# Grouping heads by bank in a causal attention step: four heads for the first 128 tokens, two for the next, one for the rest

## Chip, cores and metric

The kernel runs on one core of one Trainium2 chip. The metric is the device time of one execution in microseconds (us). Before the change it is 1768.77 us, the median of 3 runs (1768.34 to 1769.28).

## The reference

Two layers of a decoder trunk work on one sequence of 512 tokens with 1024 channels, all in float32. Each layer is a SwiGLU block, a token mixer and a second SwiGLU block. The mixer runs a causal convolution over half of its channels and a differential attention with four heads over the other half. Differential attention forms two softmax maps per head and subtracts the second, scaled, from the first:

```python
def diff_attention(q, k, v, rel_bias, lam, lam_init, subln_g):
    # q, k: (B, H, 2, S, d); v: (B, H, S, 2d); H = 4, S = 512, d = 64; 128-query blocks
    ...
        s = jnp.einsum("bhmqd,bhmkd->bhmqk", qi, k).astype(jnp.float32) * scale
        s = s + bias[None, :, None]
        s = jnp.where((dist >= 0)[None, None, None], s, -1e30)
        p = jax.nn.softmax(s, axis=-1)
        a = p[:, :, 0] - lam * p[:, :, 1]
        return jnp.einsum("bhqk,bhkd->bhqd", a.astype(v.dtype), v)
    ...
    o = rms_norm(o, subln_g) * (1.0 - lam_init)

def reference(...):
    for l in range(DEPTH):                      # 2
        x = x + 0.5 * swiglu(rms_norm(x, ffn1_norm[l]), ...)
        a, g, q, k, v = jnp.split(rms_norm(x, mix_norm[l]) @ w_in[l], splits, axis=-1)
        conv_out = conv_module(a, g, conv_w[l], conv_b[l], conv_norm[l])
        ...
        diff_out = diff_attention(q, k, v, rel_bias, lam, lam_init, subln_norm[l])
        x = x + jnp.concatenate([conv_out, diff_out], axis=-1) @ w_out[l]
        x = x + 0.5 * swiglu(rms_norm(x, ffn2_norm[l]), ...)
    return x
```

## The kernel before

The activations stay on the chip. Weights are streamed from memory and split into two parts each, so that large products run as several passes on the tensor engine (PE). Nearly all of the time goes to the SwiGLU blocks. The change touches the function `mixer` alone, which runs once per layer.

In `mixer`, queries, keys and values are projected, normalised and turned into `qz`, `kt` and `vv`. The 512 tokens are four blocks of 128 queries, numbered `i` = 0 to 3. Block `i` looks only at the first `W = (i + 1) * 128` keys, so a score product for one head and one of its two maps is 128 x W: 512 columns for the last block, 384, 256, and 128 for the first.

The attention is a pipeline of steps. Before, a step is one block and one head, 16 steps in all, with the last block first (`steps`). The function `attend(n)` issues the score and softmax work of step n (`softmaxes`), the transposes of step n - 2 (`keys_first`), the value products of step n - 3 (`values`), and the output of a block five steps behind its last head (`block_out`).

- `softmaxes` (L949): two score products, one for each map (L958), into two banks of PSUM, the tensor engine's output memory. A bank holds 512 float32 values per partition. For each map, VectorE (DVE) adds the bias and finds a running minimum (L962), and ScalarE (ACT) takes the exponential and its sum (L966). The first map goes to the tile `e0`, the second stays in its bank. A reciprocal (L969) and a small product (L971) form the factor, and L972 adds the scaled second map to the first.
- `keys_first` (L975): i + 1 transposes of 128 x 128 on PE into one bank (L979), and one ACT copy of all of them to `at` (L981).
- `values` (L984): i + 1 products for the head (L988) into its quarter of a bank that all four heads share. After the last head come the norm of the block (L995 to L1003) on ACT, DVE and GpSimd (POOL).
- `block_out` (L1011): four transposes (L1015), an ACT copy (L1017) and a DVE operation (L1018) that write the block's part of the output projection's input.

The banks come from tags, with a number of buffers each. The score banks have the tags `sc` and `po`, two buffers each; the block outputs have `mm`, two; the transposes `tp`, one; the convolution and the row sums `y`, one:

```python
    BANKS = {"mm": 2, "sc": 2, "po": 2, "tp": 1, "y": 1}

    def bank(tag, name):
        return psum.tile([P, 512], F32, tag=tag, name=name, bufs=BANKS[tag])
```

The pipeline stands between the value projection and the output projection (`ps_out`, L200 to L204 and L1065), which uses the banks `sc` and `po` too. The projection works first on the attention half for the later 256 tokens, then on the convolution half for all tokens, then on the attention half for the first 256. The convolution's taps (L902 to L931) and its norm (L933 to L943) run on DVE, ACT and POOL during the attention.

Each engine runs its instructions in a fixed order. A planner makes that order when the program is built: it walks the program with estimated durations and gives a free engine the ready instruction that stands earliest in program order, except where an order is pinned. It also places the semaphores between engines.

Of the kernel before, what the change touches and what calls it, by code (L numbers as in the profile page):

```python
# [23 lines left out]
NT = SEQ // P  # L24
# [7 lines left out]
HEADS = 4  # L32
HD = 64
VD = 2 * HD
# [36 lines left out]
def trunk(ctx: ExitStack, tc: tile.TileContext, xt, par, lamv, relb, onehot,  # L71
          gu1, dn1, wag, wqkv, wout, gu2, dn2, out):
    nc = tc.nc
    V, S, G, T = nc.vector, nc.scalar, nc.gpsimd, nc.tensor

    const = ctx.enter_context(tc.tile_pool(name="const", bufs=1))
    small = ctx.enter_context(tc.tile_pool(name="small", bufs=2))
# [11 lines left out]
    def bank(tag, name):  # L89
        return psum.tile([P, 512], F32, tag=tag, name=name, bufs=BANKS[tag])  # L90
# [121 lines left out]
    for l in range(DEPTH):  # L212
        pt = const.tile([P, NPAR], F32, tag=f"par{l}", name=f"par{l}")
# [572 lines left out]
    def mixer(l, pr, after, begun):  # L786
        with tc.tile_pool(name="mix", bufs=1) as mp, tc.tile_pool(name="mt", bufs=2) as mt:
# [155 lines left out]
                    V.scalar_tensor_tensor(cl[:, c, :], z, hg, f32(ch[:, c, :]), op0=ALU.mult, op1=ALU.subtract)  # L943


            steps = [(i, h) for i in reversed(range(NT)) for h in range(HEADS)]
            sums, pos, maps, ats = {}, {}, {}, {}

            def softmaxes(i, h):  # L949
                W = (i + 1) * P  # L950
                tq = slice(i * P, W)
                if h == 0:
                    sums[i] = small.tile([P, 2, HEADS], F32, tag="sums", name="sums")
                scs = [bank(tag, "ps_sc")[:, :W] for tag in ("sc", "po")]
                e0 = mt.tile([P, SEQ], F32, tag="e0", name="e", bufs=4)[:, :W]
                sm = sums[i]
                for m in range(2):
                    T.matmul(scs[m], qz[:, m, h, tq], kt[:, h, :W], start=True, stop=True)  # L958

                for m, (sc, e) in enumerate(zip(scs, (e0, scs[1]))):  # L960
                    mn = small.tile([P, 1], F32, tag=f"mn{m}", name="mn")
                    V.tensor_tensor_reduce(  # L962
                        out=e, in0=sc, in1=bias[:, h, SEQ - W :], scale=1.0, scalar=3e38,
                        op0=ALU.add, op1=ALU.min, accum_out=mn,
                    )
                    S.activation(e, e, AF.Exp, bias=mn, scale=-1.0, accum_out=sm[:, m, h : h + 1])  # L966

                r2 = small.tile([P, 1], F32, tag="r2", name="r2")
                V.reciprocal(r2, sm[:, 1, h : h + 1])  # L969
                c2 = small.tile([P, 1], F32, tag="c2", name="c2")  # L970
                V.tensor_scalar(c2, r2, nlam[l], sm[:, 0, h : h + 1], op0=ALU.mult, op1=ALU.mult)  # L971
                V.scalar_tensor_tensor(e0, scs[1], c2, e0, op0=ALU.mult, op1=ALU.add)  # L972
                maps[i, h] = e0

            def keys_first(i, h):  # L975
                pt = bank("tp", "ps_at")
                for j in range(i + 1):
                    t = slice(j * P, (j + 1) * P)
                    T.transpose(pt[:, t], maps[i, h][:, t], ident)  # L979
                at = mt.tile([P, SEQ], F32, tag="at", name="at")  # L980
                S.activation(at[:, : (i + 1) * P], pt[:, : (i + 1) * P], AF.Copy)  # L981
                ats[i, h] = at

            def values(i, h):  # L984
                if h == 0:
                    pos[i] = bank("mm", "ps_o")
                for j in range(i + 1):
                    T.matmul(pos[i][:, h * VD : (h + 1) * VD], ats[i, h][:, j * P : (j + 1) * P], vv[:, j, h, :],  # L988
                             start=j == 0, stop=j == i)
                if h < HEADS - 1:  # L990
# [31 lines left out]
            def attend(n):  # L1022
                if n < len(steps):
                    softmaxes(*steps[n])
                if 2 <= n < len(steps) + 2:
                    keys_first(*steps[n - 2])
                if 3 <= n < len(steps) + 3:
                    values(*steps[n - 3])
                if n >= 5 and steps[n - 5][1] == HEADS - 1:
                    block_out(steps[n - 5][0])  # L1030

            for c in range(CT - 1):
# [157 lines left out]
```

## Time and profile before

| | |
|---|---|
| median of 3 runs | 1768.77 us (1768.34 to 1769.28) |
| the profiled execution | 1769.0 us, its span 1767.2 us |
| granted PE clock | 1.00 |
| PE busy | 1758.8 us, 11852 matmul rows |
| DVE busy | 1472.1 us, 2646 instructions |
| ACT busy | 1037.1 us, 1955 instructions |
| POOL busy | 515.7 us, 497 instructions |
| first score product of the attention, layer 1 and 2 | 452.0 us, 1329.5 us after the start |

A row of the profile names the line of the kernel, the engine, the operation, the tiles written and read, the shape, and how often it came. Times are from one profiled execution. A float32 score product appears as two PE rows. Rows of PE overlap, since a product starts while the one before it is draining, so distances between starts say more of PE's speed than durations. "Idle before" names the time for which an engine had nothing running ahead of an instruction, and what ended it.

### The profile page before, as it was taken

The numbers are of one execution on the slowest core, as the hardware profiler recorded it, in microseconds if no ns is written. First come the engines' busy times: TensorE is split into PE (matmuls) and PEld (weight loads), VectorE is DVE, ScalarE is ACT, GpSimd is POOL, SyncE is SP. The second block draws the span as 40 slices with busy tenths as digits, with TensorE's granted clock in tenths as the row PEclk, the third lists the DMA queues.
The fourth block names the chain that finished last, engine by engine and source line by source line (L and its number), as shares of the span: only waits on it lengthen the run. The fifth ranks groups of instructions, "written<-read, shape, count | busy, mean of one in ns | idle before, by whom it ended". The sixth has DMA issues, their size and how long they took to land.

```text
span 1767.2 us, 32964 instructions
## 1 busy us (share of the span) xinstructions
PE 1758.8 (100%) x11852; PEld 1621.2 (92%) x11852; DVE 1472.1 (83%) x2646; ACT 1037.1 (59%) x1955; POOL 515.7 (29%) x497
## 2 busy tenths in 40 slices
PE   9999999999999999999999999999999999999998
PEld 7799999988788899999988999999887888999998
DVE  7969888969877969989987798999698678698887
ACT  6546566755865436566644565666559554465664
POOL 1011112169970011212200121121798600112122
PEclk9999999999999999999999999999999999999999
DMA  7457777533223457677544576776231234576774
GB/s 229 129 138 185 172 188 190 138 120 100 68 78 114 126 129 178 171 198 179 141 143 111 147 177 172 198 166 166 91 114 49 96 102 139 134 183 163 201 183 127
DMA packets 166613, 257.78 MB, mean 146 GB/s; under 512 B 19271, under 2 KB 63318, under 8 KB 166448
## 3 DMA queue, kind: packets, MB, share of 16 engines
q1 hardware_dynamic: 129600, 201.25, 35.5%
q0 software_dynamic: 36416, 54.12, 18.7%
q8 instruction: 93, 1.52, 0.4%
q14 instruction: 72, 0.59, 0.1%
q10 hardware_dynamic: 432, 0.29, 0.1%
HBM read 253.48 MB, written 3.42 MB: 145 GB/s over the span
## 4 chain that ended last, share of the span: by engine, by line
PE 97%; DVE 1%; POOL 1%; ACT 1%; issue 0%; DVEq 0%; POOLq 0%
PE ps_pair L434 37%; PE ps_pair L523 18%; PE ps_pair L200 9%; PE ps_pair L203 9%; PE ps_pair L204 9%; PE ps_out L200 2%; PE ps_out L203 2%; PE ps_out L204 2%; PE ps_pair L842 2%; PE ps_pair L843 2%; PE ps_pair L841 2%; PE ps_sc L958 1%; PE ps_v L872 1%; PE ps_v L873 1%; PE ps_v L871 1%; POOL wlo L102 0%
## 5 line engine op out<-in xcount | busy, mean ns | idle before, releaser
L101 ACT ACTIVATE whi<-wraw 128x512 fp32r<-128x512 f32 x744 | 452.9, 627 | 397.4 <-PE ps_pair L203 166.3
L102 DVE TENSOR_TENSOR wlo<-wraw,whi 128x512 fp32r<-128x512 f32 x640 | 426.2, 685 | 111.5 <-ACT whi L101 104.2
L160 POOL DMA_DIRECT2D wsum<-in_gu x128 | 112.0, 904 | 700.4 <-DMA wsum<-in_gu 270.7
L434 PE MATMUL ps_pair<-acth,wlo 128*128 128x256 f32 x1024 | 289.8, 283 | 0.0
L434 PE MATMUL ps_pair<-actl,whi 128*128 128x256 f32 x1024 | 289.8, 283 | 0.0
L434 PE MATMUL ps_pair<-acth,whi 128*128 128x256 f32 x1024 | 289.8, 283 | 0.0
L434 PE MATMUL ps_pair<-th,whi 128*128 128x256 f32 x768 | 217.3, 283 | 0.0
L434 PE MATMUL ps_pair<-tl,whi 128*128 128x256 f32 x768 | 217.3, 283 | 0.0
L434 PE MATMUL ps_pair<-th,wlo 128*128 128x256 f32 x768 | 217.3, 283 | 0.0
L200 PE MATMUL ps_pair<-acth,whi 128*128 128x512 f32 x512 | 200.7, 394 | 0.3 <-DVE gs L653 0.3
L203 PE MATMUL ps_pair<-actl,whi 128*128 128x512 f32 x512 | 199.7, 390 | 0.0
L204 PE MATMUL ps_pair<-acth,wlo 128*128 128x512 f32 x512 | 199.3, 390 | 0.0
L434 PEld LDWEIGHTS ps_pair<-actl,whi 128*128 128x128 f32 x1024 | 196.6, 192 | 0.2
L434 PEld LDWEIGHTS ps_pair<-acth,whi 128*128 128x128 f32 x1024 | 196.6, 192 | 0.2
L434 PEld LDWEIGHTS ps_pair<-acth,wlo 128*128 128x128 f32 x1024 | 196.6, 192 | 0.0
L160 POOL DMA_DIRECT2D wsum<-in_dn x112 | 98.9, 1112 | 269.4 <-DMA wsum<-in_dn 55.7
L434 PEld LDWEIGHTS ps_pair<-th,whi 128*128 128x128 f32 x768 | 147.5, 192 | 0.0
L434 PEld LDWEIGHTS ps_pair<-tl,whi 128*128 128x128 f32 x768 | 147.5, 192 | 0.0
L434 PEld LDWEIGHTS ps_pair<-th,wlo 128*128 128x128 f32 x768 | 147.5, 192 | 0.0
L102 POOL TENSOR_TENSOR wlo<-wraw,whi 128x512 fp32r<-128x512 f32 x104 | 137.4, 1345 | 30.4 <-ACT whi L101 19.4
L523 PE MATMUL ps_pair<-hh,whi 128*128 128x256 f32 x512 | 144.9, 283 | 0.0
L523 PE MATMUL ps_pair<-hl,whi 128*128 128x256 f32 x512 | 144.9, 283 | 0.0
(209 smaller groups left out, 4446.5 us busy)
## 6 DMA issues: line engine op xcount, KB each, us to landing
wraw<-in_gu SPq DMA_DIRECT2D x280, 256.0 KB, 3.4
wsum<-in_gu SPq DMA_DIRECT2D x128, 256.0 KB, 3.7
wsum<-in_gu POOLq DMA_DIRECT2D x128, 256.0 KB, 4.7
wraw<-in_dn SPq DMA_DIRECT2D x68, 256.0 KB, 3.4
wraw<-in_wqkv SPq DMA_DIRECT2D x48, 256.0 KB, 2.7
wraw<-in_wout SPq DMA_DIRECT2D x48, 256.0 KB, 2.7
wraw<-in_dn SPq DMA_DIRECT2D x64, 128.0 KB, 4.0
wraw<-in_wag SPq DMA_DIRECT2D x32, 256.0 KB, 3.0
```

Of the source, the lines that this page charges most:

```text
L101: S.activation(hi, raw, AF.Copy)
L102: (eng or V).tensor_tensor(out=lo, in0=raw, in1=f32(hi), op=ALU.subtract)
L160: nc.gpsimd.dma_start(dst[:, to], src, accum_op=ALU.add)
L200: first = T.matmul(ps, wh, xh, start=start, stop=False)
L203: T.matmul(ps, wh, xl, start=False, stop=False)
L204: T.matmul(ps, wl, xh, start=False, stop=stop)
L434: mm = T.matmul(ps, l, r, start=first and i == j == 0, stop=False, skip_group_check=True)
L523: mm = T.matmul(ps, s[:, f], r, start=side not in self.begun, stop=False, skip_group_check=True)
L841: T.matmul(ps[n], xh[:, t], wh, start=k == 0, stop=False)
L842: T.matmul(ps[n], xh[:, t], wl, start=False, stop=False)
L843: T.matmul(ps[n], xl[:, t], wh, start=False, stop=k == KT - 1)
L871: T.matmul(ps, xh[:, t], wh, start=k == 0, stop=False)
```

## The change

A step becomes one block and a range of heads: one head for the blocks of 512 and 384 keys, two heads for the block of 256, four for the block of 128. There are 11 steps per layer instead of 16. All heads of a step share the two score banks, one tile `e0`, one bank of transposes, one copy and one pair of reciprocal and product. Bias, exponential and combination are still issued once for each head and map. The small product is now a scalar-tensor-tensor operation on as many columns as there are heads, and the minima have four buffers per map instead of two. The distances in `attend` are the same in steps.

```diff
-            steps = [(i, h) for i in reversed(range(NT)) for h in range(HEADS)]
+            steps = []
+            for i in reversed(range(NT)):
+                g = (4, 2, 1, 1)[i]
+                steps += [(i, range(h, h + g)) for h in range(0, HEADS, g)]
...
-            def softmaxes(i, h):
-                W = (i + 1) * P
+            def softmaxes(i, hs):
+                W, g = (i + 1) * P, len(hs)
...
-                scs = [bank(tag, "ps_sc")[:, :W] for tag in ("sc", "po")]
-                e0 = mt.tile([P, SEQ], F32, tag="e0", name="e", bufs=4)[:, :W]
+                scs = [
+                    bank(tag, "ps_sc")[:, : g * W].rearrange("p (n w) -> p n w", n=g) for tag in ("sc", "po")
+                ]
+                e0 = mt.tile([P, SEQ], F32, tag="e0", name="e", bufs=4)[:, : g * W]
+                e0 = e0.rearrange("p (n w) -> p n w", n=g)
                 sm = sums[i]
                 for m in range(2):
-                    T.matmul(scs[m], qz[:, m, h, tq], kt[:, h, :W], start=True, stop=True)
+                    for n, h in enumerate(hs):
+                        T.matmul(scs[m][:, n], qz[:, m, h, tq], kt[:, h, :W], start=True, stop=True)
 
                 for m, (sc, e) in enumerate(zip(scs, (e0, scs[1]))):
-                    mn = small.tile([P, 1], F32, tag=f"mn{m}", name="mn")
-                    V.tensor_tensor_reduce(
-                        out=e, in0=sc, in1=bias[:, h, SEQ - W :], scale=1.0, scalar=3e38,
-                        op0=ALU.add, op1=ALU.min, accum_out=mn,
+                    for n, h in enumerate(hs):
+                        mn = small.tile([P, 1], F32, tag=f"mn{m}", name="mn", bufs=4)
+                        V.tensor_tensor_reduce(
+                            out=e[:, n], in0=sc[:, n], in1=bias[:, h, SEQ - W :], scale=1.0, scalar=3e38,
+                            op0=ALU.add, op1=ALU.min, accum_out=mn,
+                        )
+                        S.activation(e[:, n], e[:, n], AF.Exp, bias=mn, scale=-1.0, accum_out=sm[:, m, h : h + 1])
+
+                h = slice(hs[0], hs[-1] + 1)
+                r2 = small.tile([P, HEADS], F32, tag="r2", name="r2")[:, :g]
+                V.reciprocal(r2, sm[:, 1, h])
+                c2 = small.tile([P, HEADS], F32, tag="c2", name="c2")[:, :g]
+                V.scalar_tensor_tensor(c2, r2, nlam[l], sm[:, 0, h], op0=ALU.mult, op1=ALU.mult)
+                for n in range(g):
+                    V.scalar_tensor_tensor(
+                        e0[:, n], scs[1][:, n], c2[:, n : n + 1], e0[:, n], op0=ALU.mult, op1=ALU.add
                     )
-                    S.activation(e, e, AF.Exp, bias=mn, scale=-1.0, accum_out=sm[:, m, h : h + 1])
-
-                r2 = small.tile([P, 1], F32, tag="r2", name="r2")
-                V.reciprocal(r2, sm[:, 1, h : h + 1])
-                c2 = small.tile([P, 1], F32, tag="c2", name="c2")
-                V.tensor_scalar(c2, r2, nlam[l], sm[:, 0, h : h + 1], op0=ALU.mult, op1=ALU.mult)
-                V.scalar_tensor_tensor(e0, scs[1], c2, e0, op0=ALU.mult, op1=ALU.add)
-                maps[i, h] = e0
+                maps[i, hs] = e0
 
-            def keys_first(i, h):
+            def keys_first(i, hs):
                 pt = bank("tp", "ps_at")
-                for j in range(i + 1):
-                    t = slice(j * P, (j + 1) * P)
-                    T.transpose(pt[:, t], maps[i, h][:, t], ident)
+                for n in range(len(hs)):
+                    for j in range(i + 1):
+                        t = (n * (i + 1) + j) * P
+                        T.transpose(pt[:, t : t + P], maps[i, hs][:, n, j * P : (j + 1) * P], ident)
+                W = len(hs) * (i + 1) * P
                 at = mt.tile([P, SEQ], F32, tag="at", name="at")
-                S.activation(at[:, : (i + 1) * P], pt[:, : (i + 1) * P], AF.Copy)
+                S.activation(at[:, :W], pt[:, :W], AF.Copy)
...
+                for n, h in enumerate(hs):
+                    for j in range(i + 1):
+                        t = (n * (i + 1) + j) * P
+                        T.matmul(pos[i][:, h * VD : (h + 1) * VD], ats[i, hs][:, t : t + P], vv[:, j, h, :],
+                                 start=j == 0, stop=j == i)
+                if hs[-1] < HEADS - 1:
                     return
...
-                if n >= 5 and steps[n - 5][1] == HEADS - 1:
+                if n >= 5 and steps[n - 5][1][-1] == HEADS - 1:
                     block_out(steps[n - 5][0])
```

More of the change, by code (lines that the diff above doesn't have):

```diff
@@ L951, in softmaxes @@
                 tq = slice(i * P, W)
-                if h == 0:
+                if hs[0] == 0:
                     sums[i] = small.tile([P, 2, HEADS], F32, tag="sums", name="sums")
-                scs = [bank(tag, "ps_sc")[:, :W] for tag in ("sc", "po")]
-                e0 = mt.tile([P, SEQ], F32, tag="e0", name="e", bufs=4)[:, :W]
+                scs = [
+                    bank(tag, "ps_sc")[:, : g * W].rearrange("p (n w) -> p n w", n=g) for tag in ("sc", "po")
+                ]
+                e0 = mt.tile([P, SEQ], F32, tag="e0", name="e", bufs=4)[:, : g * W]
@@ L982, in keys_first, with values @@
-                ats[i, h] = at
-            def values(i, h):
-                if h == 0:
+                S.activation(at[:, :W], pt[:, :W], AF.Copy)
+                ats[i, hs] = at
+            def values(i, hs):
+                if hs[0] == 0:
                     pos[i] = bank("mm", "ps_o")
[L987 to L990, printed above, removed]
+                for n, h in enumerate(hs):
[4 more added lines that the diff above has]
+                if hs[-1] < HEADS - 1:
```

## The prediction

> **What bounds the kernel now.** I read the engine totals first, then the chain in order of time, then the busy time by stretches inside the token mixer, and last each engine's timeline there.
>
> ```profile
> span 1767.2 us, 32964 instructions
> ...
> PE 1758.8 (100%) x11852; PEld 1621.2 (92%) x11852; DVE 1472.1 (83%) x2646; ACT 1037.1 (59%) x1955; POOL 515.7 (29%) x497
> ```
>
> PE is busy in all but 8.4 us of the span (1767.2 - 1758.8). The change alters no matrix product: the scores, transposes and value products keep their number and widths. It can move the time only through moments in which PE waits, so the first question is how much PE loses around the attention. A busy row is not proof of full speed, so I count starts instead. The next row is from the chain in order of time and gives the undisturbed pitch of long products.
>
> ```profile
> 407.79 0.46 PE ps_pair L841 x2
> ```
>
> A 512-wide row takes 0.23 us from start to start. PE's timeline in the first mixer, columns start, duration, line, shape, count and the idle time before it:
>
> ```profile
> 479.94 1.06 PE L988 MATMUL ps_o<-vv,at 128*128 128x128 f32 x8
> 480.83 1.24 PE L958 MATMUL ps_sc<-kt,qz 128*128 128x384 f32 x4
> 481.91 0.49 PE L979 MATMUL ps_at<-ident,e 128*128 128x128 f32 x3
> ...
> 482.93 1.23 PE L958 MATMUL ps_sc<-kt,qz 128*128 128x256 f32 x4
> 484.03 0.55 PE L979 MATMUL ps_at<-ident,e 128*128 128x128 f32 x3
> ...
> 493.49 0.71 PE L988 MATMUL ps_o<-vv,at 128*128 128x128 f32 x4 [0.53 <-ACT at L981]
> ...
> 495.42 0.39 PE L200 MATMUL ps_out<-acth,whi 128*128 128x256 f32 x1
> ```
>
> Undisturbed, a 128-wide row takes (480.83 - 479.94)/8 = 0.111 us. The four score rows at 480.83 (two 384 wide, two 256 wide, merged in one row) take 1.08 us, so by width a 256-wide one has 0.216 us. From 482.93 on it is different: four 256-wide rows take 484.03 - 482.93 = 1.10 us, not 0.86, the mark of a wait that shows as no idle time: two restarts of about 0.1 us. The busy time by stretches, and two of PE's rows by shape in the first stretch:
>
> ```profile
> 482.90:497.50 14.60, 13.48 (x92) 10.98 (x91) 14.25 (x58) 12.95 (x46) 7.20 (x8) 1.00 0.01 2
> 1360.25:1374.85 14.60, 13.50 (x92) 10.97 (x91) 14.23 (x58) 12.95 (x46) 7.21 (x8) 1.00 0.01 2
> ```
>
> ```profile
> L958 PE MATMUL ps_sc<-kt,qz 128*128 128x256 f32 x10 | 3.3, 430 | 0.4 <-DVE e L972 0.4
> ...
> L291 PE MATMUL ps_spread<-diag,ones_r 128*128 128x512 f32 x2 | 1.0, 594 | 0.0
> ```
>
> Columns of the stretches: length, then busy time and rows of PE, weight loads, DVE, ACT, POOL, and the clock. In 14.60 us PE starts 92 rows. At their pitches that is 10 x 0.216 + 2 x 0.23 + 80 x 0.111 = 11.5 us of work, so **about 3.1 us is lost per layer**, and the second layer's row is the same to 0.02 us. Here DVE is busy 14.25 of 14.60 us (98%), ACT 12.95 (89%): the loop scores, bias, exponential, combination, transpose, copy is paced by DVE, and PE idles behind it. This is the stretch of the 256- and 128-wide blocks, the ones that the change regroups. Over two layers 6.2 us is the most that the change can win.
>
> **The change part by part.** *Small instructions removed.* Per layer 16 steps become 11. Each step has one reciprocal (L969) and one product (L971) on DVE.
>
> ```profile
> L971 DVE TENSOR_SCALAR c<-r,nlam,sums 128x1 f32<-128x1 f32 x7 | 1.9, 270 | 0.1
> ...
> L962 DVE DVE_READ_ACCUMULATOR2_ANT mn<- 128x1 f32 x13 | 1.5, 114 | 0.0
> ...
> L969 DVE RECIPROCAL r<-sums 128x1 f32<-128x1 f32 x7 | 1.1, 155 | 0.0
> ...
> L962 DVE CUSTOM_DVE_ANT_0 ps_sc<-ps_sc,bias 128x128 f32<-128x128 f32 x3 | 0.9, 289 | 0.0
> ...
> L972 DVE SCALAR_TENSOR_TENSOR e<-ps_sc,c,e 128x128 f32<-128x128 f32 x1 | 0.4, 351 | 0.0
> ```
>
> A pair costs 155 + 270 = 425 ns; the stretch holds seven of them (one for a 384-wide step, four for the second block, two for the first). Five pairs go per layer, 2.1 us. In the stretch itself seven become three (the 384-wide one and two grouped steps; the last group ends behind it, as its heads do now): 4 x 0.425 = **1.7 us off DVE**. The product becomes a scalar-tensor-tensor on 1 to 4 columns; the trace has none so narrow. Its bounds are the 155 ns of the reciprocal and the 351 ns of the 128-wide one at L972; I take the 270 ns of the operation that it replaces. That shift is at most 0.1 us on eleven instructions, and can go either way. Nothing else goes from DVE: bias additions and combinations stay one per head and map.
>
> *Copies merged on ACT.*
>
> ```profile
> L981 ACT ACTIVATE at<-ps_at 128x256 f32<-128x256 f32 x4 | 1.5, 379 | 0.8 <-PE ps_at L979 0.8
> ...
> L966 ACT ACTIVATION_READ_ACCUMULATOR ps_sc<-ps_sc,mn 128x1 f32 x7 | 1.4, 203 | 0.0
> ...
> L966 ACT ACTIVATE ps_sc<-ps_sc,mn 128x128 f32<-128x128 f32 x3 | 1.0, 339 | 0.5 <-DVE rowv L272 0.5
> ...
> L981 ACT ACTIVATE at<-ps_at 128x128 f32<-128x128 f32 x1 | 0.3, 278 | 0.1
> ```
>
> Four 256-wide copies (1.52 us) become two 512-wide ones, four 128-wide (1.11 us) become one. A 512-wide copy of the same line takes
>
> ```profile
> 476.50 0.59 ACT L981 ACTIVATE at<-ps_at 128x512 f32<-128x512 f32 x1
> ```
>
> so 2.63 us becomes 1.77, 0.86 us less. ACT is not the last one here (89%), so I put this at nothing; DVE's load covers it. If DVE became the faster one, ACT's 12.95 us would still be 1.65 us below the stretch's length.
>
> *Waits removed.* A score product waits until the combination of two steps earlier has freed its bank.
>
> ```profile
> PEld ps_sc L958 <- DVE e L972: 1.3, 4, 0.6
> ```
>
> With two heads in a bank the wait before the third and the fourth head of the second block disappears, and the four of the first block become one. Of the roughly 0.1 us that a matmul loses when it restarts, I count two fewer that DVE's relief doesn't already contain: 0.2 us. The transposes' single bank is filled and copied three times instead of eight for these blocks, so the exchange that ends at 493.49 (value products that wait for the copy of their transposes) occurs less often; that is inside the 1.7 us, not beside it.
>
> *Waits added.* A transposition of a group can start only when its last head is combined. Behind it in PE's queue stand the value products and then the output projection. The price is between nothing, if the queue's order puts other products ahead, and the latency of a whole group. For the four-head group the second map is bias, its accumulator, exponential and its accumulator for each head. Where these run strictly in turn, that is 4 x (0.289 + 0.114 + 0.339 + 0.203) = 3.8 us, then 0.43 us for the pair and 4 x 0.351 = 1.4 us: 5.6 us where one head now needs 1.7. I take nothing for the forecast, since from 495.42 on the projection of the later tokens lies ready beside it, and keep the difference, 3.9 us, as the bad end.
>
> A rule is to be weighed here. The rows above cannot tell whether DVE and ACT may work on two heads of one bank at once, since each bank now holds one head. The Trainium skill, page "PSUM — Partial Sum Buffer", section "PSUM bank collisions raise a hardware error", says that two engines must not access one bank in the same partitions at the same time, disjoint columns included, and that software has to keep them apart. By this rule the strict turn, 3.8 us, is what the group's second map takes; without it the exponentials alone, 4 x 0.54 = 2.2 us, would set it and the bad end would be 1.6 us less. No row here shows either.
>
> *More score buffers* (four minima per map) take no time of their own: no row of the trace waits for that tile.
>
> **The sum.** 1.7 + 0.2 = 1.9 us per layer, 3.8 us for both. The profiled execution took 1769.0 us around a span of 1767.2, so 1765.2 for it; the median of the runs is 0.23 us lower, so **1765.0 us**. Ends of the forecast: 1.05 us per layer if half of DVE's 1.7 us is lost to its own waits, 3.1 us if PE's loss vanishes: 1762.6 to 1766.7.
>
> **The rivals.** *Rival 1, the change is hidden (about 1768.8, give or take 1.5).* PE's fill at the end of the stretch is the projection, which needs block 2's output, through a chain that the change leaves alone:
>
> ```profile
> 487.49 0.83 PE L988 MATMUL ps_o<-vv,at 128*128 128x128 f32 x6
> ...
> 494.68 0.69 ACT L1017 ACTIVATE acth<-ps_o,gsub 128x512 fp32r<-128x512 f32 x1
> ```
>
> From the last head's value products of that block to the projection's start at 495.42 it takes 7.9 us. The groups' scores and softmaxes come ahead of this chain in program order: eight heads instead of five. If that delays it by what DVE's relief gives, 1.7 us, PE only idles at another place. For it: the chain's instructions queue on the full DVE and ACT. Against it: its own work is far below 7.9 us, so it is itself stretched by the load that falls.
>
> *Rival 2, the four-head group holds up PE (1772.8 to 1774.7).* If the queue places the group's transposes and value products ahead of projection rows, and the second map goes in strict turn, PE stops until the fourth head is combined. Of the 3.9 us of extra latency other ready products can cover a part; with all of it exposed and 1.9 us won, each layer is 2.0 us longer: 1772.8. A two-head group has one more turn too, at least the 0.945 us of a 128-wide one (the bracket above); with one of the two exposed in each layer the time is 1774.7. It decides as soon as over 1.9 us per layer is exposed. Against it: PE loses nothing now while the first block's last heads run beside the projection. For it: one transposition now waits for eight alternations, where an error in the planned order adds up. The strict turn is what the rule of the page named above would bring about.
>
> **How the numbers follow.** A measurement of this kernel can tell about 0.2% (3.5 us) from no change, so faster means under 1765.2, slower over 1772.3. Forecast 0.60, of which 0.42 lies under 1765.2 and 0.18 above it; rival 1 0.14, within; rival 2 0.26, slower. That makes 0.42, 0.32 and 0.26. The forecast's own range is 1762.6 to 1766.7; the range over the cases reaches from 1762.2, a little below the forecast's end, to 1774.5 in rival 2.
>
> **What would show it.** Right: in the same stretch the reciprocals and products fall from seven each to three or four, PE's rows need 1 to 1.5 us instead of 3.1 above their pitch, the waits for L972 halve, and the projection starts earlier. Rival 1: fewer small DVE rows, but the projection starts as late and PE idles ahead of it. Rival 2: a single PE wait of 2 us or more ahead of the first block's transposes, released by DVE's combination, with bias rows and exponentials of one bank strictly in turn. The forecast is wrong if PE's loss in the stretch stays at 3 us or grows, or if the time moves outside the mixers.

## The result: slower, 1774.5 us

The changed kernel takes 1774.52 us (median of 7 runs, 1773.88 to 1775.67). The kernel before takes 1768.77 us. The ratio is 1.0033, 95% interval 1.0023 to 1.0043: **slower by 5.75 us**, where 3.8 us faster was forecast. The first two lines answer to the page's head of before:

```profile
span 1772.8 us, 32932 instructions
...
PE 1759.8 (99%) x11852; PEld 1621.1 (91%) x11852; DVE 1478.9 (83%) x2626; ACT 1035.7 (58%) x1945; POOL 515.3 (29%) x497
```

VectorE runs 20 instructions fewer, as the change says (2626 for 2646), and yet it is busy 6.8 us longer (1478.9 for 1472.1). That says where to look: some instruction got slower by more than the removed ones were worth. The view of one tile, for the small product's output `c` (L980, L971 before), with duration minimum, median and maximum in ns:

```profile
L980 DVE SCALAR_TENSOR_TENSOR c<-r,nlam,sums x22: 210/676/2431, 457.9 to 1380.8; 128x1 f32<-128x1 f32 x16, 128x2 f32<-128x2 f32 x4, 128x4 f32<-128x4 f32 x2
```

An operation on one column takes between 0.21 and 2.43 us. The same view of the kernel before:

```profile
L971 DVE TENSOR_SCALAR c<-r,nlam,sums x32: 259/272/275, 458.3 to 1379.8; 128x1 f32<-128x1 f32 x32
```

There all 32 lie within 16 ns. The longest one of the changed kernel, in the second layer, is followed here across three engines. VectorE's timeline (start, duration, line, operation), then GpSimd's, then TensorE's:

```profile
1356.54 0.16 DVE L978 RECIPROCAL r<-sums 128x1 f32<-128x1 f32 x1 [0.55 <-ACT ps_sc L974]
1356.73 2.43 DVE L980 SCALAR_TENSOR_TENSOR c<-r,nlam,sums 128x1 f32<-128x1 f32 x1
1359.09 0.55 DVE L970 CUSTOM_DVE_ANT_0 ps_sc<-ps_sc,bias 128x384 f32<-128x384 f32 x1
```

```profile
1354.17 3.76 POOL L102 TENSOR_TENSOR wlo<-wraw,whi 128x512 fp32r<-128x512 f32 x3
1357.87 2.62 POOL L913 TENSOR_TENSOR yp<-yp,prod 128x512 f32<-128x512 f32 x2
```

```profile
1360.23 0.91 PE L965 MATMUL ps_sc<-kt,qz 128*128 128x384 f32 x2 [1.64 <-DVE e L982]
```

The product starts at 1356.73, when the third of GpSimd's three weight splits starts (1354.17 + 2 x 1.25 = 1356.67), and ends at 1356.73 + 2.43 = 1359.16, when the first of the two L913 rows ends (1357.87 + 1.31 = 1359.18). It waited for two GpSimd instructions in a row. The combination (L982) stands behind it on VectorE, TensorE's next scores wait for that combination's bank, and TensorE idles 1.64 us. The kernel before has no such wait there. The other long ones end in the same way: of the 22 products 15 take over 0.4 us, and each of these ends within 0.02 us of the end of a GpSimd instruction.

The two layers of the changed kernel make a comparison in which nothing is edited, since every engine runs the attention of both in the same order. The same product and the same scores in the first layer:

```profile
476.98 1.22 DVE L980 SCALAR_TENSOR_TENSOR c<-r,nlam,sums 128x1 f32<-128x1 f32 x1
```

```profile
479.26 0.91 PE L965 MATMUL ps_sc<-kt,qz 128*128 128x384 f32 x2 [0.42 <-DVE e L982]
```

The product is 1.21 us longer in the second layer (2.43 against 1.22), and TensorE's wait behind it 1.22 us longer (1.64 against 0.42). Here the wait passes to TensorE in full.

The busy time by stretches, the same stretch as in the prediction, and TensorE's waits from 440 to 520 us:

```profile
482.90:497.50 14.60, 12.27 (x87) 9.97 (x85) 13.67 (x50) 12.62 (x44) 7.31 (x9) 1.00 0.01 2
```

```profile
PE ps_o L1004 <- ACT at L995: 1.4, 2, 0.7
PE ps_o L1031 <- DVE ov L1019: 0.7, 2, 0.4
PE ps_sc L965 <- DVE e L982: 0.4, 1, 0.4
```

TensorE starts 87 rows instead of 92. Before, it waited only 0.9 us in those 80 us.

### The profile page after: what moved, and what is told of

It is laid out like the page before. It is cut to its first block, busy times and chain, and to the rows that moved or that the text cites. A ratio compares the mean times of both kernels' runs of the same rounds, so it can differ in the third digit from the quotient of the medians.

```text
span 1772.8 us, 32932 instructions
## 1 busy us (share of the span) xinstructions
PE 1759.8 (99%) x11852; PEld 1621.1 (91%) x11852; DVE 1478.9 (83%) x2626; ACT 1035.7 (58%) x1945; POOL 515.3 (29%) x497
## 4 chain that ended last, share of the span: by engine, by line
PE 94%; DVE 3%; ACT 2%; issue 0%; DVEq 0%
PE ps_pair L434 36%; PE ps_pair L523 18%; PE ps_pair L200 9%; PE ps_pair L203 9%; PE ps_pair L204 9%; PE ps_out L204 2%; PE ps_out L200 2%; PE ps_out L203 2%; PE ps_pair L842 2%; PE ps_pair L841 2%; PE ps_pair L843 2%; DVE ps_y L927 1%; DVE c L980 1%; ACT e L974 0%; PE ps_v L872 0%; PE ps_v L873 0%
```

## The experiments

The first theory is A: the small product became a scalar-tensor-tensor with two tensor operands in SBUF (reciprocal and sums), and such an instruction waits until GpSimd's running instruction ends. The first rivals are B (the grouped score banks make VectorE and ScalarE take turns and the group is late) and C (the groups' heads stand ahead of block 2's chain to the projection). D, E and F came from the results and are told at their place.

A measure is used throughout. **TensorE's loss** is the sum, over all its matmul starts from 440 to 520 and from 1320 to 1400 us, of the time to the next start less one pitch for each kind of row, the same in all kernels and read from the kernel before: 0.111 us for a 128-wide row, 0.216, 0.323 and 0.429 us for scores 256, 384 and 512 wide, 0.120 and 0.227 us for other rows 256 and 512 wide. All kernels of this study in one table:

| kernel | median us | ratio to before, 95% interval | TensorE's loss, us |
|---|---|---|---|
| before | 1768.77 | | 6.64 |
| after | 1774.52 | 1.0033, 1.0023 to 1.0043 | 12.53 |
| ts_g1111 | 1768.58 | 0.9999, 0.9990 to 1.0008 | 6.66 |
| b_stt | 1772.85 | 1.0022, 1.0014 to 1.0031 | 9.91 |
| ts | 1773.79 | 1.0028, 1.0018 to 1.0039 | 11.80 |
| r2psum | 1770.26 | 1.0008, 0.9999 to 1.0017 | 8.05 |
| r2p_gap2 | 1769.98 | 1.0007, 0.9998 to 1.0016 | 8.05 |
| r2p_phased | 1769.06 | 1.0000, 0.9991 to 1.0009 | 6.71 |
| r2p_g4111 | 1770.07 | 1.0007, 0.9998 to 1.0016 | 8.13 |
| r2p_g1211 | 1772.49 | 1.0020, 1.0011 to 1.0029 | 10.46 |
| mix | 1770.83 | 1.0011, 1.0002 to 1.0020 | 8.31 |
| mix_phased | 1772.26 | 1.0019, 1.0010 to 1.0028 | 9.93 |
| mix_g1211 | 1769.42 | 1.0004, 0.9995 to 1.0013 | 7.39 |
| mix_g4111 | 1773.72 | 1.0027, 1.0016 to 1.0038 | 11.95 |
| b_gap1 | 1771.57 | 1.0015, 1.0006 to 1.0024 | 8.96 |
| r2p_g1111 | 1776.30 | 1.0042, 1.0029 to 1.0054 | 14.38 |
| r2psum_at1 | 1770.27 | 1.0009, 1.0000 to 1.0017 | 8.06 |
| r2p_phased_at1 | 1768.90 | 1.0000, 0.9991 to 1.0009 | 6.38 |

The median less the loss lies between 1761.8 and 1762.9 us in every row, while the medians spread over 7.7 us. So most of what moves the time is what TensorE loses inside the two mixers, as the prediction took it, and the question is which wait makes it.

**b_stt: the operation alone, without any group.** The kernel before, with one line changed:

```diff
-  V.tensor_scalar(c2, r2, nlam[l], sm[:, 0, h : h + 1], op0=ALU.mult, op1=ALU.mult)
+  V.scalar_tensor_tensor(c2, r2, nlam[l], sm[:, 0, h : h + 1], op0=ALU.mult, op1=ALU.mult)
```

> The kernel before with only the small product changed from tensor-scalar to scalar-tensor-tensor, still one head per step. Theory A: 16 products per layer instead of 11 run into POOL; with the mean excess of 0.4 us seen after, DVE loses about 6 us per layer in a stretch where it paces PE, and the time is 1774 to 1780 us. Theory B: no group, so no change: 1768 to 1770 us.

Measured: 1772.85 us, 4.1 us more than before. The tile view, then one row of VectorE's timeline and one of GpSimd's:

```profile
L971 DVE SCALAR_TENSOR_TENSOR c<-r,nlam,sums x32: 210/220/1232, 457.8 to 1382.8; 128x1 f32<-128x1 f32 x32
```

```profile
476.82 1.23 DVE L971 SCALAR_TENSOR_TENSOR c<-r,nlam,sums 128x1 f32<-128x1 f32 x1
```

```profile
474.28 3.76 POOL L102 TENSOR_TENSOR wlo<-wraw,whi 128x512 fp32r<-128x512 f32 x3
```

The product ends at 478.05, GpSimd's three splits at 478.04. The planner laid out every engine of this kernel as before until two 128-wide scores are moved, in the row that starts at 486.46 us; nothing is in another order ahead of that. So the two kernels can be laid side by side there. Value products of the same two heads, in b_stt and before:

```profile
474.71 1.06 PE L988 MATMUL ps_o<-vv,at 128*128 128x128 f32 x8
...
485.49 0.83 PE L988 MATMUL ps_o<-vv,at 128*128 128x128 f32 x6
```

```profile
475.19 1.06 PE L988 MATMUL ps_o<-vv,at 128*128 128x128 f32 x8
...
484.41 0.83 PE L988 MATMUL ps_o<-vv,at 128*128 128x128 f32 x6
```

From the first to the second it is 9.22 us before and 10.78 us in b_stt: **1.56 us more in this stretch of one layer, with no instruction moved**. The four products between them take 3.07 us there (1.23, 0.99, 0.21 and 0.64) and 1.09 us before, so most of what VectorE got in addition reached TensorE. Over both layers TensorE loses 3.3 us more than before; this and the 4.1 us contain what the orders do behind the point where they part. Theory B, by which the product changes nothing (1768 to 1770 us), fails here. A's wait is there, but A had its cost larger, 1774 to 1780 us.

**r2psum: the same groups, with the wait taken away.** The changed kernel, with its reciprocal (`r2`) written into the bank of the first maps, which is used up by then. The small product then reads one operand from PSUM:

```diff
-  r2 = small.tile([P, HEADS], F32, tag="r2", name="r2")[:, :g]
+  r2 = scs[0][:, 0, :g]
```

> The kernel after, with the reciprocal written into the first map's score bank, whose scores are used up by then, so that the small product keeps its form and reads one tensor from PSUM and one from the on-chip memory. Theory A: the product takes 0.2 to 0.3 us each time, whatever POOL does; the time falls to 1766 to 1771 us (the bank is held longer, which can cost some of it). If the width or kind of the operation were slow by itself, and not its two inputs, it would stay at 0.2 to 2.4 us and the time near 1774. Theory B: 1773 to 1776.

Measured: 1770.26 us, 4.3 us less than the changed kernel and inside A's 1766 to 1771 us. The tile view and the stretch:

```profile
L980 DVE SCALAR_TENSOR_TENSOR c<-ps_sc,nlam,sums x22: 202/218/220, 458.0 to 1379.0; 128x1 f32<-128x1 f32 x16, 128x2 f32<-128x2 f32 x4, 128x4 f32<-128x4 f32 x2
```

```profile
482.90:497.50 14.60, 13.23 (x92) 11.21 (x90) 13.00 (x51) 13.06 (x46) 8.51 (x10) 1.00 0.01 2
```

Every product now takes at most 220 ns, and 22 of them 4.7 us instead of 15.3. The Trainium skill, page "SBUF — State Buffer", section "Who interferes with whom", gives the rule: a VectorE instruction with two SBUF inputs contends with a GpSimd instruction that reads SBUF, one of the two then blocks fully, and an instruction with at most one SBUF input, outside the modes that use both of VectorE's ports for one tensor, does not contend. The two tile rows agree: 2431 ns at most with two SBUF operands, 220 ns with one.

The row of the stretch carries a second result. VectorE's load fell by 1.25 us (14.25 to 13.00), where the forecast had 1.7 us. TensorE starts the same 92 rows as before, and over both mixers it loses 8.05 us against 6.64. The relief came, and no gain on TensorE came with it.

**ts and ts_g1111: the product as it was before.** In ts the groups stay, and each head of a group has its own tensor-scalar; ts_g1111 is the same with one head in every step:

```diff
-  V.scalar_tensor_tensor(c2, r2, nlam[l], sm[:, 0, h], op0=ALU.mult, op1=ALU.mult)
+  for n in range(g):
+      V.tensor_scalar(c2[:, n : n + 1], r2[:, n : n + 1], nlam[l], sm[:, 0, hs[n] : hs[n] + 1], ...)
```

```diff
-  g = (4, 2, 1, 1)[i]
+  g = (1, 1, 1, 1)[i]
```

> The kernel after, with the small product as one tensor-scalar operation per head (L971's form of before: one tensor input, two scalars) instead of one scalar-tensor-tensor per step. Grouping stays. Theory A (the scalar-tensor-tensor has two tensor inputs in the on-chip memory and waits until POOL's running instruction ends; in the trace after it takes 0.21 to 2.43 us, 7.3 and 8.0 us for 11 of them per layer against 0.27 each before): the product falls back to about 0.27 us, DVE wins 2.9 us per layer net of five more instructions, and the time falls to 1766 to 1769.5 us. Theory B (the groups' latency, bias and exponential in turn in one bank, stops PE; the product is a bystander): within 1.5 us of the kernel after, 1773 to 1775.

> The kernel after with tensor-scalar products and every group cut to one head: the steps of before, in the new code, with four minima buffers per map. A control for the code around the groups. All theories: 1768 to 1770 us, the time of before.

Measured: 1773.79 and 1768.58 us. Without groups the new code is the kernel before: every engine runs the same instructions in the same order. With groups and the old product, the wait for GpSimd is gone (the product takes 262 to 276 ns), and still 5.0 us are lost. Theory A had 1766 to 1769.5 us for ts and missed; B's 1773 to 1775 us holds it. So taking the wait away gave 4.3 us in r2psum and only 0.7 us here, and both kernels have an order of their own. The product's tile view in ts, then TensorE's, VectorE's and ScalarE's timelines:

```profile
L981 DVE TENSOR_SCALAR c<-r,nlam,sums x32: 262/271/276, 457.9 to 1377.6; 128x1 f32<-128x1 f32 x32
```

```profile
498.32 0.50 PE L994 MATMUL ps_at<-ident,e 128*128 128x128 f32 x2 [0.68 <-DVE e L984]
...
500.34 1.13 PE L1006 MATMUL ps_o<-vv,at 128*128 128x128 f32 x8 [0.83 <-DVE actl L1036]
```

```profile
494.24 0.28 DVE L970 CUSTOM_DVE_ANT_0 ps_sc<-ps_sc,bias 128x128 f32<-128x128 f32 x1
...
495.11 0.30 DVE L970 CUSTOM_DVE_ANT_0 ps_sc<-ps_sc,bias 128x128 f32<-128x128 f32 x1
...
495.99 0.30 DVE L970 CUSTOM_DVE_ANT_0 ps_sc<-ps_sc,bias 128x128 f32<-128x128 f32 x1
...
499.45 0.75 DVE L1036 SCALAR_TENSOR_TENSOR actl<-ps_o,gsub,acth 128x512 fp32r<-128x512 f32 x1
```

```profile
494.62 0.34 ACT L974 ACTIVATE ps_sc<-ps_sc,mn 128x128 f32<-128x128 f32 x1 [0.90 <-DVE mn L970]
...
495.50 0.34 ACT L974 ACTIVATE ps_sc<-ps_sc,mn 128x128 f32<-128x128 f32 x1
...
496.38 0.34 ACT L974 ACTIVATE ps_sc<-ps_sc,mn 128x128 f32<-128x128 f32 x1 [0.42 <-DVE mn L970]
...
497.73 0.68 ACT L1035 ACTIVATE acth<-ps_o,gsub 128x512 fp32r<-128x512 f32 x1
```

In the four-head group's bank, bias and exponential come strictly in turn (494.24, 494.62, 495.11, 495.50, 495.99, 496.38), 0.88 us a head, and the group's transposes at 498.32 wait 0.68 us for its combination. That is the turn of theory B. That it makes the loss is not shown: the projection rows behind these transposes need block 2's `acth`, which ends at 498.41 (497.73 + 0.68; before, 495.37), and the second idle time, 0.83 us, is put down to block 2's `actl`, which ends at 500.20. Block 2's output is late here as well, which is theory C. In the changed kernel itself no transpose of the first block waits for L982, so B's wait is not among its losses.

**r2p_phased and r2p_gap2: B against C.** With the product repaired, 1.5 us are left. The first kernel breaks the turn, the second moves the four-head group behind block 2's chain:

```diff
   for n, h in enumerate(hs):
       mn = ...
       V.tensor_tensor_reduce(out=e[:, n], ...)
-      S.activation(e[:, n], e[:, n], AF.Exp, bias=mn, ...)
+      mns.append(mn)
+  for n, h in enumerate(hs):
+      S.activation(e[:, n], e[:, n], AF.Exp, bias=mns[n], ...)
```

```diff
+  if i == 0:
+      steps += [None] * 2      # attend skips empty steps
```

> The changed kernel with the reciprocal in PSUM, and with all the biases of a group issued before all its exponentials, so that VectorE and ScalarE no longer take turns head by head in a bank. Theory B (the turn sets the loss): the second maps of the four-head group take about 2 us instead of 3.8, the combinations and transposes come 1.5 us sooner, and the time falls by 1 to 2 us from 1770.26 to 1768.5 to 1769.2. Theory C (block 2's chain is what the projection waits for): VectorE has four biases in a row ahead of block 2's work where one head's work stood before; the time stays at 1769.8 to 1771.5 us.

> The changed kernel with the reciprocal written into the used-up bank of the first maps (so that the small product reads one operand from SBUF and one from PSUM), and with two empty steps ahead of the four-head group of the first block, so that blocks 2 and 1 have made their outputs before the group's biases come up on VectorE. Without the empty steps that kernel took 1770.26 us, 1.5 us over the kernel before. Theory C (block 2's chain, its sum of squares to its split outputs, stands behind the heads that the groups bring forward; with the reciprocal in PSUM the first output bank began at 496.83 us of the span and before at 495.42, 1.4 us a layer): VectorE meets the sum of squares and the scaling of block 2 with one head's work less ahead of them, the output projection begins about as early as before, and the time falls to 1768.0 to 1769.2 us. Theory B (the group's own strict turn of VectorE and ScalarE in one bank, 0.95 us a head, makes its transposes late and TensorE waits for them): the group starts later still, so the wait stays or moves behind the projection's start, 1770 to 1772 us.

Measured: 1769.06 and 1769.98 us. The groups of instructions by line show the turn and its end; the bias rows of r2psum, then of r2p_phased:

```profile
L970 DVE CUSTOM_DVE_ANT_0 ps_sc<-ps_sc,bias 128x512 f32<-128x512 f32 (+3 forms) x32 | 15.8, 493 | 3.1 <-ACT ps_sc L974 2.2 <-PE ps_sc L965 0.8
```

```profile
L972 DVE CUSTOM_DVE_ANT_0 ps_sc<-ps_sc,bias 128x512 f32<-128x512 f32 (+3 forms) x32 | 15.8, 494 | 1.2 <-PE ps_sc L965 0.8
```

VectorE's 2.2 us of waiting for ScalarE in the shared bank are gone, and the time is 1.2 us lower, as B had it (1768.5 to 1769.2); C's 1769.8 to 1771.5 missed. For r2p_gap2 C had 1768.0 to 1769.2 and missed; B's 1770 to 1772 begins right above the time. But the next runs show that a difference of this size proves little.

**r2p_g4111, r2p_g1211, r2p_g1111: which group costs.** r2psum with other group sizes:

```diff
-  g = (4, 2, 1, 1)[i]
+  g = (4, 1, 1, 1)[i]      # r2p_g4111
+  g = (1, 2, 1, 1)[i]      # r2p_g1211
+  g = (1, 1, 1, 1)[i]      # r2p_g1111
```

> The changed kernel with the reciprocal in PSUM, with only the first block's heads grouped by four and all the others taken one at a time. Theory C: block 2's chain meets the four heads of the first group and block 1's last heads one by one, as in the kernel before except for the group; a part of the 1.5 us remains, 1768.8 to 1769.6 us. Theory B: the four-head group alone carries the loss, 1769.8 to 1770.5 us.

> The changed kernel with the reciprocal in PSUM, with only the second block's heads grouped by two and the others taken one at a time. Theory B: without the four-head group nothing is lost, 1768.4 to 1769.0 us. Theory C: the two-head groups bring one head forward at most, so most of the loss goes, 1768.6 to 1769.4 us; a time of 1769.8 or more would mean that the two-head groups are the cause, and neither theory has that.

> The changed code with one head in every step, the product as in the change, and the reciprocal in the used-up bank of the first maps. No head is grouped; what differs from the kernel before is that the first bank is held until the product, and another order. Theory D (the hold of the bank costs): 1770 to 1772 us, TensorE's scores waiting for the small product in blocks 3 to 1. Theory E (the groups are what loses): 1768.4 to 1769.2 us.

Measured: 1770.07, 1772.49 and 1776.30 us. r2p_g4111 agrees with C's figure to 0.5 us and lies in B's. r2p_g1211 lies in neither: both had at most 1769.4 us. And without any group this repair is slowest of all, where theory E (the groups' coarse steps are what loses) had the time of before. TensorE's waits over the whole span of r2p_g1111 name a reason:

```profile
PE ps_out L200 <- DVE c L980: 1.6, 2, 0.8
PE ps_sc L965 <- DVE c L980: 1.5, 4, 0.5
```

Scores and projection wait for the small product itself. With the reciprocal in the first maps' bank, that bank comes free only after the product and no longer after the first bias. My repair had a price of its own (theory D), and the kernel of heads taken alone lies 7.5 us over the kernel before, beyond the 1 to 3 us that D expected; the waits of the two rows are 3.1 us of it. The part of it that r2psum pays is not known.

**mix, mix_phased, mix_g1211, mix_g4111: the repair without that price.** Groups keep the reciprocal in the bank; heads alone keep it in SBUF and use the tensor-scalar:

```diff
+  if g == 1:
+      r2 = small.tile([P, HEADS], F32, tag="r2", name="r2")[:, :g]
+      ...
+      V.tensor_scalar(c2, r2, nlam[l], sm[:, 0, h], op0=ALU.mult, op1=ALU.mult)
+  else:
       r2 = scs[0][:, 0, :g]
```

> The changed kernel, in which the groups write their reciprocal into the used-up bank of the first maps, and the heads taken one at a time keep the reciprocal in SBUF and the product by a tensor-scalar, as in the kernel before. The kernel with every reciprocal in the bank took 1770.26 us; with it a one-head step gives its first bank back only after the product and no longer after the first bias (the trace of the same with two-head groups alone shows a score matmul that waits for the small product). Theory D (what was left after the product's repair was this longer hold of the bank in the 16 to 24 one-head steps, and not the groups): 1768.0 to 1768.9 us. Theory B (the groups' strict turn in the bank): 1769.6 to 1770.5 us, since the groups are as they were.

> The same, with all the biases of a group ahead of all its exponentials. With every reciprocal in the bank this order took 1769.06 us. Theory D: about the same as without this order, or a few tenths less, 1767.6 to 1768.8 us. Theory B: 1 us under the kernel without this order, 1768.4 to 1769.2 us. A time under 1768.2 us would beat the kernel before.

> The same repair, with only the second block's heads grouped, by two. With every reciprocal in the bank this grouping took 1772.49 us. Theory D: the hold of the bank was its loss, 1768.3 to 1769.2 us. Theory B and C: the loss is none of the bank's in the one-head steps, so 1771 us or more.

> The same repair, with only the first block's heads grouped, by four. With every reciprocal in the bank this grouping took 1770.07 us. Theory D: 1768.2 to 1769.0 us. Theory B: 1769.5 to 1770.3 us, as the four-head groups are unchanged.

Measured: 1770.83, 1772.26, 1769.42 and 1773.72 us. D's ranges are missed by all four: by 0.2 us for the two-head groups alone, which did get faster (1772.49 to 1769.42), and by 2 to 5 us for the others. B's are missed too. mix is no faster than r2psum, mix_phased is 3.2 us slower than r2p_phased, mix_g4111 3.7 us slower than r2p_g4111, though a price was taken out of each. Breaking the turn, worth 1.2 us above, costs 1.4 us here. Something else of this size changes from kernel to kernel. TensorE's waits in the first mixer point to no common place: mix waits 1.1 us for a combination, mix_phased 1.3 us for a copy, mix_g4111 1.3 us for the projection's bank.

**b_gap1: the order alone.** Theory F takes that something for the order in which the planner lays out each kernel. The kernel before, with one empty step ahead of block 0 (`attend` skips it): the same instructions on every engine, in another order.

```diff
+  steps[-HEADS:-HEADS] = [None] * 1
```

> The kernel before, with one empty step ahead of the first block's four heads: the same instructions on every engine, but the planner lays them out in another order. Theory F (what the grouped kernels differ by among themselves, 1769 to 1774 us, comes in good part from the order that the planner makes of each edit): this order too moves the time by 0.5 us or more, to anywhere from 1768 to 1772 us. Theory E (with one head a step the pipeline is fine-grained enough that any order holds, and the groups' coarser steps are what loses): 1768.4 to 1769.2 us.

Measured: 1771.57 us, **2.8 us slower with nothing changed but the order**. Its stretch of the prediction's table looks better than before, and the loss lies elsewhere; the stretch, then the first row of TensorE's waits over the span:

```profile
482.90:497.50 14.60, 13.59 (x94) 11.20 (x94) 14.08 (x58) 12.71 (x46) 6.89 (x9) 1.00 0.01 2
```

```profile
PE ps_out L200 <- DVE x L1066: 1.6, 2, 0.8
```

The projection waits 0.8 us a layer for the addition that frees its bank, right behind two value products that this order put there. Theory E, by which any order holds with one head a step, had at most 1769.2 us and failed on this kernel; F had 1768 to 1772 us. So an order can move the time as much as these kernels differ. That it is what moved each of them is not shown.

**r2psum_at1, r2p_phased_at1: the grouped copy.** The grouped kernels with the repair show a stall of the value products behind ScalarE's one copy of a whole group (r2psum: 0.69 us at 492.26). Here it is cut into one copy a head:

```diff
-  S.activation(at[:, :W], pt[:, :W], AF.Copy)
+  w = (i + 1) * P
+  for n in range(len(hs)):
+      S.activation(at[:, n * w : (n + 1) * w], pt[:, n * w : (n + 1) * w], AF.Copy)
```

> The changed kernel with the reciprocal in PSUM (1770.26 us), and ScalarE's copy of a group's transposes cut into one copy a head. All grouped kernels so far have a stall of 0.85 to 1.47 us a layer of the value products behind the 512-wide copy (0.69 us) of a group. Theory E (the coarse step, here the group's copy, is what loses): the first head's copy takes about a quarter, the stall falls by about half a microsecond a layer, 1769.0 to 1769.6 us. Theory F: the new order decides, 1768.8 to 1773 us, without the stall at the copy setting it.

> The grouped kernel nearest to the kernel before (all biases ahead of all exponentials, reciprocal in PSUM, 1769.06 us), with the copy cut into one a head. Its largest stall is one of 1.17 us a layer behind a group's copy. Theory E: 0.5 us a layer less, 1767.9 to 1768.4 us, under the kernel before. Theory F: the new order decides, 1768.5 to 1773 us.

Measured: 1770.27 and 1768.90 us, unchanged within 0.2 us, where theory E had 0.5 us a layer less. TensorE's timeline of r2psum_at1:

```profile
491.79 1.16 PE L1006 MATMUL ps_o<-vv,at 128*128 128x128 f32 x8 [0.47 <-ACT at L997]
...
493.37 1.10 PE L291 MATMUL ps_spread<-diag,ones_r 128*128 128x512 f32 x2 [0.42 <-DVE diag L287]
```

The wait for the copy fell from 0.69 to 0.47 us, and the next wait, for the convolution's norm, grew from the 0.21 us of r2psum to 0.42. What was won there came back at the next wait. No version with groups beats the kernel before by more than its interval; r2p_phased_at1 comes closest to it, ratio 1.0000.

**What is shown and what stays open.** Shown: the product's two SBUF operands put waits of up to 2.43 us on VectorE, and these reach TensorE with no order changed: 1.22 us between the two layers of the changed kernel, 1.56 us in the stretch of b_stt. Added alone they cost 4.1 us. Not shown is how many of the 5.75 us they are: taken away they give back 4.3 us in r2psum and 0.7 us in ts, each with a new order, and in r2psum against the longer hold of the bank. Not settled either: the rest, 1.5 us by r2psum. Its interval (0.9999 to 1.0017) touches no change, an order alone is worth 2.8 us, and the grouped kernels without the wait span 1768.90 to 1773.79 us. So whether grouping in itself costs or wins is smaller than what the order does with it. An order held fixed while only the groups change was not tried.

## Why the prediction was wrong, point by point

*What bounds the kernel.* Right that only TensorE's loss in the mixers counts: after less before is 5.89 us of loss (12.53 - 6.64) against 5.75 us of time. **Wrong is the step from VectorE's load to time.** A share of 98% was read as the limit. In r2psum VectorE is at 89% of the stretch (13.00 of 14.60), and TensorE loses more than before, not less. Block 2's chain, from its last value products to the projection, takes 8.3 us there (488.51 to 496.83), where it took 7.9 with the fuller VectorE. Work added to VectorE does cost TensorE time (1.22 us between the layers, 1.56 us in b_stt). Work taken off it won nothing in any grouped kernel. Which wait then ends last is not shown; that the chain of results from engine to engine does, and not VectorE's load, is argued.

*Small instructions removed: 1.7 us.* The count was right and most of the relief came (1.25 us in r2psum). The step that failed is the next one, that the relief passes to TensorE: even without the product's wait, r2psum takes 1770.26 us, 5.3 us over the 1765.0 forecast.

*The product as a scalar-tensor-tensor: 155 to 351 ns, 270 taken, "at most 0.1 us on eleven instructions".* **This is the term that made the change slower.** Undisturbed it takes 210 ns, inside the bounds. Its mean was 694 ns (15.3 us / 22), and eleven of them take 7.6 us a layer where 3.0 were counted (11 x 0.27). The bounds came from widths and left out where the operands lie. The kernel before carried the warning; in the view of one tile, an operation of the same form with both tensors in SBUF:

```profile
L941 DVE SCALAR_TENSOR_TENSOR u<-th,u x6: 682/1772/1782, 503.9 to 1387.3; 128x512 f32<-128x512 f32 x6
```

The same six instructions take from 682 to 1782 ns, a spread that no width explains. I read the median of others and not this minimum and maximum.

*Copies merged, at nothing.* Not quite free: TensorE's waits for the copy rose from 0.5 to 1.4 us in the first mixer. Cutting the copy in the two repaired kernels changed the time by no more than 0.2 us; in the changed kernel it was not cut.

*Restarts, 0.2 us won.* Not found; the changed kernel adds waits.

*Waits added, none.* In the changed kernel the group's transposes do not hold TensorE at the first block, as taken. In ts they wait 0.68 us.

*The strict turn.* The rule of the Trainium skill weighed in the prediction, page "PSUM — Partial Sum Buffer", section "PSUM bank collisions raise a hardware error", agrees with the trace of ts: no bias and exponential of the group's second maps overlap, and a head takes 0.88 us where 0.945 was worked out. In r2psum VectorE's biases wait 2.2 us for ScalarE in that bank, so the program keeps the two apart; what happens where it does not, no run shows.

*Rival 1.* Its shape is in r2psum: fewer small rows, the relief given away, the projection later (496.83 against 495.42). But r2p_phased starts it later still, at 496.99, and loses nothing. The projection's start alone does not decide.

*Rival 2.* Its range, 1772.8 to 1774.7, holds the measured time, by another mechanism. The number agreed and the reason did not: its sign, a wait of 2 us or more ahead of the first block's transposes, is not in the changed kernel. That was luck. Its argument that TensorE loses nothing beside the projection was not right either: in the kernel before, the row at 495.42 starts 0.30 us later than the two transposes ahead of it need (494.90 + 2 x 0.111 = 495.12). And its upper end is 1774.7 by its own working, where the range over the cases says 1774.5; the 1762.2 at the other end is worked out nowhere.

*Not among the cases:* a tiny instruction that waits for another engine's memory access, and the price of a new order, which neither the sum nor the range had.

## What to carry to other kernels

When an instruction is exchanged for another of the same size, compare where each operand lies, not only the width: here one SBUF operand more made 0.21 us into up to 2.43. A high busy share does not price a saving: before a saving on that engine is counted, name the wait that ends last and follow the saving to it. And where a planner lays the order out anew, run an edit that changes the order alone first; differences below what it shows (2.8 us here) belong to no mechanism until an order is held.

## What the runs showed of the hardware

A one-column instruction on VectorE with two SBUF tensor operands waited for GpSimd's running instruction: 15 of the 22 in the changed kernel take over 0.4 us, and each ends within 0.02 us of the end of one, where one undisturbed takes 210 ns. Once it waited for two in a row (2.43 us, at 1356.73). At the same place of the first layer it was done after one (1.22 us, at 476.98), with the next right behind as well, so what decides this is open. GpSimd did not pay for these waits: the eight weight splits between 465 and 482 us take 1290 to 1307 ns in the changed kernel and 1282 to 1322 ns before. The scalars of a tensor-scalar, read from SBUF as well (`nlam` and `sums`), do not bring this wait: 259 to 275 ns for all 32.
